# Three more waiting turns, and sample columns written by another engine, in a hybrid decoder step on one Trainium2 core

## The chip, the cores and the metric

The kernel runs on one core of a Trainium2 chip. A core has a matrix engine (TensorE, PE in the profile), a vector engine (VectorE, DVE), a scalar engine (ScalarE, ACT), a general engine (GpSimd, POOL), a queue engine that mostly issues transfers (SyncE, SP), and DMA engines that move data between the device memory and the on-chip buffers. The metric is the device time of one execution in microseconds; lower is better.

## What is computed

One inference step of one decoder layer, for 256 prompt tokens of a new sequence and 32 sample tokens (8 sequences of 4 tokens) with cached state. The two are held side by side as 288 columns.

```python
h = rms_norm(x, norm_mix_pre)
p_rwkv, lru_x, lru_g, q, k, v = split(h @ w_in)          # 2048 -> 5888 columns
y_a = rwkv7_mix(p_rwkv, ...)      # 8 heads of 64, matrix state per head
y_b = rglru_mix(lru_x, lru_g, ...)  # gated linear recurrence, width 512
y_c = attend(q, k, v)             # 8 heads of 128, three dilated windows; the sample tokens
                                  # also read a cache of 2048 keys and values per sequence
x = x + rms_norm(concat(y_a, y_b, y_c) @ w_out, norm_mix_post)
f = square(relu(rms_norm(x, norm_ffn_pre) @ ffn_w1)) @ ffn_w2
x = x + rms_norm(f, norm_ffn_post)
```

Also returned are the new states, and the keys and values of the new tokens.

## The kernel before

**The weight stream.** All weights pass once, as 382 chunks of 512 KB: 94 of `w_in`, 32 of `w_out`, 256 of the two feed-forward matrices. For a chunk, SP issues a load into one of RW = 4 buffers `w32` (L383); ACT rounds it into one of RH = 3 slots of `ring_h` (L393); DVE subtracts to get the rest in `ring_l` (L394, called the split here); PE runs 24 products of 128x288 (L429, L430, L431 in turn). SP, ACT and DVE run ahead of PE by at most these buffers: a split for chunk n waits until chunk n - 3 is used.

**The side work.** All else of the mixing stage (RWKV, recurrence, attention) is written as Python generators. `pump` advances each of them once per chunk, after 6 of 8 steps of its products; a `yield` waits for the next turn, and its value is a cost that counts towards a budget. So a number of `yield`s is a distance in chunks between what stands before and behind it. Behind this the Tile scheduler places each instruction in the one fixed order of its engine. Each engine then runs its own list in order, and an instruction that waits holds all behind it.

**The work around the change.**
- `gen_inv(hf)` inverts small triangular blocks, for two halves of the RWKV heads. DVE does 15 steps (L855, L857), copies (L860), and SP takes the result through device memory: two stores (L863), and eight loads with 64-byte runs into `TQ` (L868). `gen_mats` waits for `R["TQ"]` to be set and multiplies by it (L897).
- `evac_qkv` takes a finished head of q, k or v from the accumulator: DVE scales all 288 columns into a tile (L1314), then GpSimd copies the 32 sample columns of it into a collecting tile `qs`, `ks` or `vs` (L1315). `evac_lru` has GpSimd fill the leading columns of the convolution input (L1179, L1180).
- `gen_sample_scores` multiplies the sample queries by the cached keys: 32 loads `in_kc` of 896 KB by GpSimd (L1376), two at a time to products (L1408). Each load is tied behind `S["mark"]`, the latest copy into a collecting tile, in the order only. Two stream buffers in `arm` hold the keys.
- `gen_sample_soft(g)` scales the sample probabilities (DVE, L1437) and transposes them on PE (L1445). `gen_sample_pv` multiplies by the cached values: 32 loads `in_vc` (L1472) to products (L1494), 56 for a pair of loads. `more_streams` adds two more buffers from the arena (called `ar` and `arx` in the profile) as soon as there is room.
- `gen_prompt_attn` does the prompt's scores (L1561, L1562), softmax (L1565 to L1579) and transposes (L1585).

Of the kernel before, what the change touches and what calls it, by code (L numbers as in the profile page):

```python
# [12 lines left out]
ALU = mybir.AluOpType  # L13
# [298 lines left out]
def build(tc, A, O):  # L312
    nc = tc.nc
    sy, dv, ac, po, pe = nc.sync, nc.vector, nc.scalar, nc.gpsimd, nc.tensor
    with ExitStack() as ctx:
# [10 lines left out]
        rs_in = cp.tile([128, NT], F32, name="rs_in")  # L326
# [16 lines left out]
        def pvc(name, i=0, n=1):  # L343
            o, _ = PV[name]
            return pv[:, o + i:o + i + n]
# [89 lines left out]
        def must(*dims, **kw):  # L435
            n = 0
            while True:
                t = arena.get(*dims, **kw)
                if t is not None:
                    return t  # L440
                n += 1
                if n > 50:
                    raise RuntimeError("arena full")
                pump(100)
# [139 lines left out]
        S = {}  # L584
# [6 lines left out]
        def aw(*dims, **kw):  # L591
            while True:
                t = arena.get(*dims, **kw)
                if t is not None:
                    return t
                yield 0

        def bk(n=1):
            while len(banks.b) < n:
                yield 0  # L600
            return [banks.get() for _ in range(n)]
# [230 lines left out]
        def gen_inv(hf):  # L832
            R = RS[hf]
            while "MA1" not in R:
                yield 0
            dm = dp.tile([128, 512], F32, name=f"dm{hf}")
            do = dp.tile([8, 16, 256], F32, name=f"do{hf}")
            TQ = yield from aw(16, 64, top=True)
            po.memset(TQ, 0.0)
            W = yield from aw(4, 16, 16, top=True)  # L840
            Dm, Ti, Qi, tmp = (W[0:64, i] for i in range(4))
            for j in range(2):
                sy.dma_start(out=dm[:, 256 * j:256 * j + 256].rearrange("p (h t) -> p h t", h=4), in_=R["MA%d" % j][:, :, 0])
            po.memset(Ti, 0.0)
            d = Ti[:, 0, 0:1]
            po.memset(bass.AP(tensor=d.tensor, offset=d.offset, ap=[list(d.ap[0]), [17, 16]]), 1.0)
            d = dm[0:1, 0:1]
            for cb_ in range(8):
                sy.dma_start(out=Dm[8 * cb_:8 * cb_ + 8],
                             in_=bass.AP(tensor=d.tensor, offset=d.offset + 16 * 512 * cb_ + 16 * (cb_ % 4),  # L850
                                         ap=[[64, 8], [512, 16], [1, 16]]))
            yield 0
            for t in range(1, 16):
                v = tmp.rearrange("p a b -> p (a b)")[:, 0:t * t].rearrange("p (c s) -> p c s", c=t)
                dv.tensor_tensor(out=v, in0=Dm[:, 0:t, t].unsqueeze(1).to_broadcast([64, t, t]),  # L855
                                 in1=Ti[:, 0:t, 0:t].rearrange("p s c -> p c s"), op=ALU.mult)
                dv.tensor_reduce(out=Ti[:, t, 0:t], in_=v, axis=mybir.AxisListType.X, op=ALU.add)  # L857
                if t % 5 == 0:
                    yield 0
            dv.tensor_copy(out=Qi, in_=Ti.rearrange("p t s -> p s t"))  # L860
            for i, src in enumerate((Ti, Qi)):
                d = do[0:1, 0:1, 0:1]
                sy.dma_start(out=bass.AP(tensor=d.tensor, offset=d.offset + 8 * 256 * i, ap=[[16 * 256, 8], [256, 8], [1, 256]]),  # L863
                             in_=src.rearrange("p a b -> p (a b)"))
            for cb_ in range(8):
                c, b4 = cb_ // 4, cb_ % 4
                d = do[cb_:cb_ + 1, 0:1, 0:1]
                sy.dma_start(out=TQ[16 * cb_:16 * cb_ + 16, :, 16 * b4:16 * b4 + 16],  # L868
                             in_=bass.AP(tensor=d.tensor, offset=d.offset, ap=[[16, 16], [256, 16], [1, 16]]))
            arena.put(W)  # L870
            R["TQ"] = TQ
            yield 0

        def gen_mats(hf, j):
            R = RS[hf]
# [300 lines left out]
        def evac_lru(i, ps):  # L1176
            if i < 4:
                t = must(XW)
                po.memset(t[:, 0:3], 0.0)  # L1179
                po.tensor_copy(out=t[:, 259:283], in_=pvc("conv", 24 * i, 24))  # L1180
                dv.tensor_tensor(out=t[:, 3:259], in0=ps[:, 0:256], in1=rs_in[:, 0:256], op=ALU.mult)
                dv.tensor_tensor(out=t[:, 283:315], in0=ps[:, 256:288], in1=rs_in[:, 256:288], op=ALU.mult)
                sy.dma_start(out=O["o_conv_p"][:, i], in_=t[:, 256:259])
                sy.dma_start(out=O["o_conv_s"][:, i], in_=t[:, 291:315])
                xbt[i] = t
            else:
                t = must(NT)
                dv.tensor_tensor(out=t, in0=ps, in1=rs_in, op=ALU.mult)
                gbt[i - 4] = t
# [120 lines left out]
        def evac_qkv(which, i, ps):  # L1310
            if i == 0:
                S[which + "s"] = must(8, NS)
            t = must(NT)
            dv.tensor_tensor(out=t, in0=ps, in1=rs_in, op=ALU.mult)  # L1314
            S["mark"] = po.tensor_copy(out=S[which + "s"][:, i], in_=t[:, 256:288])  # L1315
            QKV[which, i] = t
            if which == "v":
                S["late"] = True
            S[which + "n"] = i + 1
            if which != "q":  # L1320
                sy.dma_start(out=O["o_" + which][:, i], in_=t)
# [108 lines left out]
        def gen_sample_soft(g):  # L1430
            SS = S["SS"]
            st_ = yield from aw(4)
            dv.tensor_reduce(out=st_[:, 0:1], in_=SS[:, g], axis=mybir.AxisListType.X, op=ALU.max)
            dv.tensor_scalar(out=st_[:, 0:1], in0=st_[:, 0:1], scalar1=-1.0, scalar2=None, op0=ALU.mult)
            ac.activation(out=SS[:, g], in_=SS[:, g], func=AF.Exp, bias=st_[:, 0:1], accum_out=st_[:, 1:2])
            dv.reciprocal(out=st_[:, 2:3], in_=st_[:, 1:2])
            dv.tensor_scalar(out=SS[:, g], in0=SS[:, g], scalar1=st_[:, 2:3], scalar2=None, op0=ALU.mult)  # L1437
            PT = yield from aw(8, 128)
            yield 0
            for half in range(2):  # L1440
                b, = yield from bk(1)
                for q in range(4):
                    kt = 4 * half + q
                    n = 128 if kt < 7 else 32
                    pe.transpose(b[0:n, 128 * q:128 * q + 128], SS[:, g, 128 * kt:128 * kt + n], ident)  # L1445
                if half == 0:
                    ac.activation(out=PT[:, 0:4], in_=b.rearrange("p (a b) -> p a b", a=4), func=AF.Copy)
                else:
                    ac.activation(out=PT[:, 4:7], in_=b[:, 0:384].rearrange("p (a b) -> p a b", a=3), func=AF.Copy)
                    ac.activation(out=PT[0:32, 7], in_=b[0:32, 384:512], func=AF.Copy)  # L1450
                banks.put(b)
                yield 0.5
            arena.put(st_)
            S["PT%d" % g] = PT

        def gen_sample_pv():
# [18 lines left out]
            for g in range(2):  # L1475
                while "PT%d" % g not in S:
                    yield 0
# [57 lines left out]
        def gen_prompt_attn():  # L1535
# [14 lines left out]
            for h0 in range(0, 8, 2):  # L1550
# [28 lines left out]
                    dv.tensor_scalar(out=PF[:, e, sl], in0=P[:, e, sl, ::-1], scalar1=s_[:, 8 + i:9 + i], scalar2=None, op0=ALU.mult)  # L1579
                yield 1.4  # L1580
                PT = yield from aw(2, 3, 128)
                bs = yield from bk(2)
                for e in range(2):
                    for i in range(3):
# [41 lines left out]
        for hf in range(2):  # L1626
            gens += [gen_rwkv(hf), gen_form(hf), gen_inv(hf), gen_mats(hf, 0), gen_mats(hf, 1), gen_chain(hf), gen_gn(hf)]
        gens += [gen_lru()]

        def evac_in(s, ps):  # L1630
            i = ORDER[s]
            if i < 14:
                evac_rwkv(i, ps)
            elif i < 22:
                evac_lru(i - 14, ps)
            else:
                w, h = "qkv"[(i - 22) // 8], (i - 22) % 8
                if "att" not in S:
                    S["att"] = True
                    gens.extend([gen_sample_scores(), gen_sample_pv(), gen_prompt_attn(), gen_prompt_pv()])  # L1640
                evac_qkv(w, h, ps)
# [92 lines left out]
        ps = psm.tile([128, NT], F32, name="mm", tag="mm")  # L1734
# [84 lines left out]
        ps = psm.tile([128, NT], F32, name="mm", tag="mm")  # L1819
# [3 lines left out]
        ps = psm.tile([128, NT], F32, name="mm", tag="mm")  # L1823
# [26 lines left out]
```

## Time and profile before

| | |
|---|---|
| median of 3 runs | 1458.4 us (1455.09, 1458.4, 1458.5) |
| profiled execution | 1457.43 us, of which 1455.4 us span and 2.0 us outside it |
| mean granted TensorE clock | 0.985 |
| busy share of the span | PE 97%, DVE 57%, ACT 41%, POOL 5% |
| mixing stage with side work | chunks 0 to 123, to about 610 us |
| products of a chunk on PE | 24, 0.133 us apart, so 3.2 us |
| cached key load, cached value load | 7.3 us and 7.3 to 8.9 us from issue to landing (medians) |

Read it so: PE is busy nearly all the time, with one dense stream of products, so a microsecond is gained or lost only where PE stands still, or runs at a lower granted clock. The feed-forward part after 620 us is dense and is not touched by the change.

### The profile page before, as it was taken

To read this page: it belongs to the slowest core of one execution; us is meant where nothing else is said; L and a number is where in the kernel's file an instruction comes from. 1 tells how busy PE (TensorE), PEld (TensorE's weight loads), DVE (VectorE), ACT (ScalarE), POOL (GpSimd) and SP (SyncE) were. 2 spreads that over 40 slices of the span, in tenths; PEclk is the share of its full clock that TensorE was granted. 3 is DMA by queue.
4 is the path that set the end of the run, shared out by engine and by line. 5 is a ranking of instruction groups with operands and counts; after the bars stand their busy time and mean duration, and the time that the engine had idled before them with its cause. 6 is when DMAs were issued, how large, how long until landed. Compare 5 with 4: busy or idle time off the path is not lost.

```text
span 1455.4 us, 28004 instructions
## 1 busy us (share of the span) xinstructions
PE 1415.3 (97%) x11730; PEld 1342.6 (92%) x11730; DVE 834.7 (57%) x1399; ACT 595.9 (41%) x866; POOL 67.5 (5%) x159
## 2 busy tenths in 40 slices
PE   8998999899999999999999999999999999999995
PEld 8898877787788999999999999999999999999995
DVE  7795486734586756695533355544455444454555
ACT  7432422333244533664443444433344333444442
POOL 1101011111111100000000000000000000000000
PEclk9999999899999999999999999999999999999998
DMA  8546366667778974434454444444445444454442
GB/s 294 185 152 196 124 235 224 225 244 258 269 263 332 321 281 163 158 125 166 159 170 164 166 168 161 171 162 169 164 162 171 161 171 163 165 169 161 171 161 80
DMA packets 86046, 276.62 MB, mean 190 GB/s; under 512 B 22384, under 2 KB 26016, under 8 KB 83872
## 3 DMA queue, kind: packets, MB, share of 16 engines
q1 hardware_dynamic: 75136, 212.23, 42.7%
q0 software_dynamic: 9920, 60.83, 11.3%
q8 instruction: 92, 1.51, 0.4%
q10 hardware_dynamic: 864, 1.77, 0.4%
q14 instruction: 34, 0.28, 0.1%
HBM read 267.97 MB, written 6.84 MB: 189 GB/s over the span
## 4 chain that ended last, share of the span: by engine, by line
PE 70%; issue 2%; DVE 2%; DMA 2%; ACT 1%; POOL 0%; DVEq 0%; POOLq 0%
PE mm L429 22%; PE mm L431 22%; PE mm L430 22%; DMA arm<-in_vc 1%; PE bt L1494 1%; DMA arm<-in_kc 1%; PE bt L1408 0%; DVE arm L1827 0%; DVE arx L1828 0%; PE bt L425 0%; DVE ring_l L394 0%; ACT ring_h L393 0%; DMA w<-in_w_out 0%; PE bt L1612 0%; ACT L1277 0%
## 5 line engine op out<-in xcount | busy, mean ns | idle before, releaser
L394 DVE TENSOR_TENSOR ring_l<-w,ring_h 128x1024 fp32r<-128x1024 f32 (+1 forms) x382 | 465.0, 1218 | 389.7 <-ACT ring_h L393 388.9
L393 ACT ACTIVATE ring_h<-w 128x1024 fp32r<-128x1024 f32 (+1 forms) x382 | 402.9, 1055 | 593.0 <-PE mm L430 523.7
L429 PE MATMUL mm<-hh,ring_h 128*128 128x288 f32 x1984 | 598.7, 302 | 4.8 <-ACT ring_h L393 3.0
L431 PE MATMUL mm<-hh,ring_l 128*128 128x288 f32 x1984 | 592.1, 299 | 0.8 <-DVE ring_l L394 0.8
L430 PE MATMUL mm<-hl,ring_h 128*128 128x288 f32 x1984 | 592.3, 299 | 0.2 <-DVE hl L548 0.2
L429 PEld LDWEIGHTS mm<-hh,ring_h 128*128 128x128 f32 x1984 | 373.7, 188 | 15.9 <-issue 7.1
L431 PEld LDWEIGHTS mm<-hh,ring_l 128*128 128x128 f32 x1984 | 374.8, 189 | 9.7 <-issue 5.5
L430 PEld LDWEIGHTS mm<-hl,ring_h 128*128 128x128 f32 x1984 | 374.4, 189 | 8.7 <-issue 5.8
L430 PE MATMUL mm<-fl,ring_h 128*128 128x288 f32 x1024 | 302.1, 295 | 0.0
L431 PE MATMUL mm<-fh,ring_l 128*128 128x288 f32 x1024 | 301.9, 295 | 0.0
L429 PE MATMUL mm<-fh,ring_h 128*128 128x288 f32 x1024 | 300.3, 293 | 0.0
L429 PEld LDWEIGHTS mm<-fh,ring_h 128*128 128x128 f32 x1024 | 192.5, 188 | 0.0
L430 PEld LDWEIGHTS mm<-fl,ring_h 128*128 128x128 f32 x1024 | 192.5, 188 | 0.0
L431 PEld LDWEIGHTS mm<-fh,ring_l 128*128 128x128 f32 x1024 | 192.4, 188 | 0.0
L1795 ACT ACTIVATE fh<-ft 128x288 fp32r<-128x288 f32 x64 | 28.3, 444 | 78.9 <-DVE ft L1794 78.9
L1803 DVE TENSOR_TENSOR arm<-mm,arm 128x288 f32<-128x288 f32 x48 | 22.0, 458 | 51.2 <-PE mm L431 51.2
L1796 DVE TENSOR_TENSOR fl<-ft,fh 128x288 fp32r<-128x288 f32 x64 | 29.2, 458 | 29.1 <-ACT fh L1795 29.1
L1408 PE MATMUL bt<-arm,ar 128*32 128x448 f32 x256 | 28.0, 546 | 2.6 <-DMA arm<-in_kc 2.3
L1794 DVE SCALAR_TENSOR_TENSOR ft<-mm,rt 128x288 f32<-128x288 f32 x63 | 28.3, 450 | 0.0
L1793 ACT ACTIVATE rt<-mm 128x288 f32<-128x288 f32 x63 | 24.9, 395 | 0.4 <-PE mm L431 0.4
L1702 DVE TENSOR_TENSOR ar<-mm,ar 128x288 f32<-128x288 f32 x32 | 14.5, 454 | 11.5 <-PE mm L431 11.5
L1376 POOL DMA_DIRECT2D arm<-in_kc x32 | 17.0, 531 | 70.2 <-PE bt L1408 61.4
(376 smaller groups left out, 906.9 us busy)
## 6 DMA issues: line engine op xcount, KB each, us to landing
w<-in_w SPq DMA_DIRECT2D x256, 512.0 KB
w<-in_w_in SPq DMA_DIRECT2D x91, 512.0 KB
arm<-in_kc POOLq DMA_DIRECT2D x32, 896.0 KB, 7.3
w<-in_w_out SPq DMA_DIRECT2D x32, 512.0 KB
arm<-in_vc POOLq DMA_DIRECT2D x8, 1024.0 KB, 7.4
ar<-in_vc POOLq DMA_DIRECT2D x8, 1024.0 KB, 7.3
arm<-in_vc POOLq DMA_DIRECT2D x9, 768.0 KB, 8.8
arx<-in_vc POOLq DMA_DIRECT2D x7, 768.0 KB, 8.9
```

Of the source, the lines that this page charges most:

```text
L393: ac.activation(out=h[:, lo:hi], in_=t[:, lo:hi], func=AF.Copy)
L394: dv.tensor_tensor(out=l[:, lo:hi], in0=t[:, lo:hi], in1=h[:, lo:hi].bitcast(F32), op=ALU.subtract)
L429: pe.matmul(out=ps, lhsT=h, rhs=xh, start=start, stop=False)
L430: pe.matmul(out=ps, lhsT=h, rhs=xl, start=False, stop=False)
L431: pe.matmul(out=ps, lhsT=l, rhs=xh, start=False, stop=stop)
L1376: after(po.dma_start(out=t, in_=A["kc"][seq[i]]), S["mark"])
L1408: pe.matmul(out=bh[32 * h:32 * h + 32, 0:448], lhsT=qz[:, h, b], rhs=t[:, h], start=(b == 0), stop=(b == NB - 1))
L1793: ac.activation(out=r, in_=ps, func=AF.Relu)
L1794: dv.scalar_tensor_tensor(out=f, in0=ps, scalar=0.0, in1=r, op0=ALU.max, op1=ALU.mult)
L1795: ac.activation(out=fh[:, m], in_=f, func=AF.Copy)
L1796: dv.tensor_tensor(out=fl[:, m], in0=f, in1=fh[:, m].bitcast(F32), op=ALU.subtract)
L1803: dv.tensor_tensor(out=facc[:, m], in0=ps, in1=facc[:, m], op=ALU.add)
```

## The change

It does five things. The numbers of waiting turns: in `gen_inv`, three turns pass between the issue of the loads of `TQ` and the setting of `R["TQ"]`, where before it was set at once; in `gen_sample_soft`, two turns rather than one between the scaling and the transposes; in `gen_prompt_attn`, one turn more between the scalings and the transposes. The engines: the leading columns of `evac_lru` are written by DVE; and the sample columns in `evac_qkv` are a second product by DVE straight from the accumulator, no longer a copy by GpSimd of the scaled tile, so that `S["mark"]` is now a DVE instruction.

```diff
@@ gen_inv @@
             arena.put(W)
+            for _ in range(3):
+                yield 0
             R["TQ"] = TQ
-            yield 0
@@ evac_lru @@
                 t = must(XW)
-                po.memset(t[:, 0:3], 0.0)
-                po.tensor_copy(out=t[:, 259:283], in_=pvc("conv", 24 * i, 24))
+                dv.memset(t[:, 0:3], 0.0)
+                dv.tensor_copy(out=t[:, 259:283], in_=pvc("conv", 24 * i, 24))
@@ evac_qkv @@
             dv.tensor_tensor(out=t, in0=ps, in1=rs_in, op=ALU.mult)
-            S["mark"] = po.tensor_copy(out=S[which + "s"][:, i], in_=t[:, 256:288])
+            S["mark"] = dv.tensor_tensor(out=S[which + "s"][:, i], in0=ps[:, 256:288], in1=rs_in[:, 256:288], op=ALU.mult)
@@ gen_sample_soft @@
             PT = yield from aw(8, 128)
-            yield 0
+            for _ in range(2):
+                yield 0
@@ gen_prompt_attn @@
                 PT = yield from aw(2, 3, 128)
+                yield 0
                 bs = yield from bk(2)
```

What this does to the order of the engines is shown at three places. Line numbers of the changed kernel are higher by 1 behind L868, by 2 behind L1437 and by 3 behind L1581. A place on PE is given as the number of chunks whose products stand before it: 58.00 is behind 58 times 24 of them.

**The first key loads on GpSimd.** `ar_88` and `arx` are tiles of the arena; L1392 spreads the sample queries. Before:

```order
L1315 COPY arx<-arx 128x32
L1392 COPY ar_88<-arx 128x8x4
L1315 COPY arx<-arx 128x32
L1376 DMA arm<-in_kc 128x1792 x2
L1392 COPY ar_88<-arx 128x8x4
```

After the change, in the same place:

```order
L615 COPY ar_88<-pv 128x8
L1393 COPY ar_88<-arx 128x8x4
L1377 DMA arm<-in_kc 128x1792 x2
L1393 COPY ar_88<-arx 128x8x4 x3
L1377 DMA arm<-in_kc 128x1792 x8
```

The first two loads stood behind two copies L1315 and now stand behind the first L1393 alone; eight more follow without a copy between them. On PE the first key products move from 40.33 to 38.54, the second pair from 42.83 to 39.58. The first products with `TQ` (L897, now L898) stay at 34.75.

**PE at chunk 58.** Before, one run of side products with no weight product between them:

```order
L431 MATMUL mm<-hh,ring_l 128x288
L1445 MATMUL bt<-ca,arx 128x128 x4
L897 MATMUL bt<-ar_88 64x64 x16
L1561 MATMUL bt<-ar_88,arx 128x128
L1562 MATMUL bt<-ar_88,arx 128x256
L1561 MATMUL bt<-arx 128x128
L1562 MATMUL bt<-arx 128x256
L429 MATMUL mm<-hh,ring_h 128x288
```

After the change, what stands at 57.83:

```order
L431 MATMUL mm<-hh,ring_l 128x288
L1409 MATMUL bt<-arm,ar_88 32x448 x4
L898 MATMUL bt<-ar_88 64x64 x8
L429 MATMUL mm<-hh,ring_h 128x288
L430 MATMUL mm<-hl,ring_h 128x288
L431 MATMUL mm<-hh,ring_l 128x288
L429 MATMUL mm<-hh,ring_h 128x288
L430 MATMUL mm<-hl,ring_h 128x288
L898 MATMUL bt<-ar_88 64x64 x8
```

The transposes L1447 now come at 55.54 and 55.79, the prompt's transposes at 56.54 and 56.75, the prompt's scores L1563 from 58.25 on; key products now stand at 57.21 and 57.83, and a pair of value products at 56.21.

On DVE, the part just ahead of this place. Before, between two splits (L394, of the chunks 53 and 54):

```order
L394 TENSOR_TENSOR ring_l<-w_2345,ring_h 128x1024
L1138 SCALAR_TENSOR_TENSOR ar_88<-bt,ar_88 128x288 x2
L1149 RECIPROCAL ar_88<-ar_88 128x288 x2
L1120 TENSOR_TENSOR ar_88<-bt,ar_88 128x512
L1150 TENSOR_TENSOR ar_88<-ar_88 128x576
L1122 TENSOR_TENSOR ar_88<-ar_88 128x512
L1153 TENSOR_SCALAR ar_88<-ar_88,pv 128x288 x2
L1114 TENSOR_TENSOR ar_88<-ar_88,ca 128x512
L1155 TENSOR_TENSOR ar_88<-ar_88 128x576
L778 TENSOR_TENSOR ar_88<-bt,ar_88 128x288
L855 TENSOR_TENSOR ar_88<-ar_88 64x1
L394 TENSOR_TENSOR ring_l<-w_2397,ring_h 128x1024
```

After the change, the start of a run of 42 instructions without a split, behind which the next split stands:

```order
L394 TENSOR_TENSOR ring_l<-w_2306,ring_h 128x1024
L1150 RECIPROCAL ar_88<-ar_88 128x288
L855 TENSOR_TENSOR ar_88<-ar_88 64x1
L1121 TENSOR_TENSOR ar_88<-bt,ar_88 128x512
L857 TENSOR_REDUCE ar_88<-ar_88 64x1
L1150 RECIPROCAL ar_88<-ar_88 128x288
L855 TENSOR_TENSOR ar_88<-ar_88 64x4
L1123 TENSOR_TENSOR ar_88<-ar_88 128x512
L857 TENSOR_REDUCE ar_88<-ar_88 64x2
L1151 TENSOR_TENSOR ar_88<-ar_88 128x576
```

The inverse's steps now lie among the reciprocals and scalings, and ten of its fifteen pairs stand in this run; before, one.

**The value loads on GpSimd.** Before, where the third and fourth buffer come in (`ar_88`, `arx`; a buffer of `arm` is one of the first two):

```order
L1472 DMA ar_88<-in_vc 128x2048
L1376 DMA arm<-in_kc 128x1792 x2
L1179 MEMSET arx 128x3
L1472 DMA arm<-in_vc 128x1536
L1472 DMA arm<-in_vc 128x2048
L1179 MEMSET arx 128x3
L1180 COPY arx<-pv 128x24
L1472 DMA arx<-in_vc 128x1536
```

After the change:

```order
L1474 DMA arm<-in_vc 128x2048
L1474 DMA arm<-in_vc 128x1536
L1474 DMA ar_88<-in_vc 128x2048
L1474 DMA arm<-in_vc 128x2048
L1474 DMA arm<-in_vc 128x1536 x2
L1474 DMA arm<-in_vc 128x2048
L1474 DMA ar_88<-in_vc 128x1536
```

All ten value loads ahead of these rows' third go to `arm`; the third buffer is first taken by the row with `ar_88`. Before, the pairs of value products stood at 59.00, 74.88, 78.21, 79.83, 80.46, 80.71, 81.75 and then every two chunks; now at 56.21, 73.88, 75.33, 78.58, 81.12, 82.50 (its second part at 82.88), 83.08 (second part 83.17), 84.75 and then every two chunks.

## Rows read from the trace of the kernel before

**Rows 1.** The page: busy time by engine; a group of instructions by line.

```profile
PE 1415.3 (97%) x11730; PEld 1342.6 (92%) x11730; DVE 834.7 (57%) x1399; ACT 595.9 (41%) x866; POOL 67.5 (5%) x159
...
L394 DVE TENSOR_TENSOR ring_l<-w,ring_h 128x1024 fp32r<-128x1024 f32 (+1 forms) x382 | 465.0, 1218 | 389.7 <-ACT ring_h L393 388.9
```

**Rows 2.** Waits of PE: in total us, times, longest us.

```profile
PE bt L897 <- DMA ar<-do: 4.3, 1, 4.3
PE bt L1494 <- DMA ar<-in_vc: 3.1, 1, 3.1
PE mm L429 <- ACT ring_h L393: 3.0, 3, 1.6
...
PE bt L1494 <- DMA arm<-in_vc: 1.1, 1, 1.1
```

**Rows 3.** Windows: length; PE, PEld, DVE, ACT, POOL busy; clock, DMA share, GB/s.

```profile
0.00:10.00 10.00, 6.07 (x31) 5.32 (x32) 3.24 (x6) 5.14 (x9) 2.81 (x20) 1.00 0.80 262
...
130.00:140.00 10.00, 5.68 (x42) 5.36 (x41) 2.91 (x3) 1.51 (x2) 1.09 (x4) 0.90 0.84 255
140.00:150.00 10.00, 10.00 (x75) 8.99 (x76) 4.25 (x7) 3.27 (x3) 1.30 (x2) 0.76 0.43 156
280.00:290.00 10.00, 6.39 (x45) 4.71 (x46) 5.11 (x12) 1.59 (x3) 0.21 (x1) 0.57 0.46 162
290.00:300.00 10.00, 9.95 (x141) 9.03 (x141) 4.35 (x13) 4.12 (x13) 1.29 (x3) 0.92 0.31 105
430.00:440.00 10.00, 6.71 (x109) 5.48 (x107) 7.15 (x11) 2.82 (x5) 1.08 (x3) 0.92 0.90 346
440.00:450.00 10.00, 9.07 (x114) 8.23 (x115) 5.47 (x19) 5.33 (x7) 2.45 (x6) 0.74 0.98 381
```

**Rows 4.** Timeline of PE at 139 us: start, length, idle before it.

```profile
139.41 0.44 PE L897 MATMUL bt<-ar 64*64 64x64 f32 x2 [4.32 <-DMA ar<-do]
```

**Rows 5.** Timeline of POOL, 120 to 130 us.

```profile
121.26 1.48 POOL L1392 COPY ar<-arx 128x32 f32<-128x32 f32 x1
128.22 1.15 POOL L1315 COPY arx<-arx 128x32 f32<-128x32 f32 x1 [5.48 <-DVE arx L1314]
129.31 1.06 POOL L1376 DMA_DIRECT2D arm<-in_kc  x2
```

**Rows 6.** Timeline of SP's queue, 126 to 142 us.

```profile
131.11 4.89 SPq L868 DMA_DIRECT2D ar<-do  x8
```

**Rows 7.** DMA queues, 134 to 136 us: packets, MB, share (q0 GpSimd's, q1 SP's).

```profile
q0 software_dynamic: 132, 0.83, 99.9%
q1 hardware_dynamic: 56, 0.01, 2.4%
```

**Rows 8.** The same, 277 to 280 us, while the other half's TQ is loaded.

```profile
q1 hardware_dynamic: 1592, 0.10, 34.5%
```

**Rows 9.** Timeline of PE at chunk 58, 281 to 290 us.

```profile
281.04 0.88 PE L1445 MATMUL bt<-ca,arx 128*128 128x128 f32 x4 [1.98 <-DVE arx L1437]
282.67 1.29 PE L897 MATMUL bt<-ar 64*64 64x64 f32 x16 [0.75 <-ACT ar L1447]
284.54 1.12 PE L897 MATMUL bt<-ar 64*64 64x64 f32 x16 [0.59 <-DVE ar L898]
286.19 0.80 PE L1561 MATMUL bt<-ar,arx 128*128 128x128 f32 x2 [0.53 <-DVE ar L898]
...
288.56 0.79 PE L1561 MATMUL bt<-arx 128*128 128x128 f32 x2 [0.71 <-DVE ar L1565]
```

**Rows 10.** Timeline of PE, a pair of value products, 427 to 430 us.

```profile
427.43 1.08 PE L1494 MATMUL bt<-ar 128*32 128x128 f32 x32
```

**Rows 11.** Timeline of POOL: the first load that refills this pair's buffers.

```profile
428.84 0.53 POOL L1472 DMA_DIRECT2D ar<-in_vc  x1 [7.88 <-PE bt L1494]
```

**Rows 12.** The line L1472, all of its 32 loads, issue to landing.

```profile
DMA to landing us min/median/max: 4.8/8.0/11.4
```

**Rows 13.** The window with the work around chunk 58.

```profile
250.00:300.00 50.00, 45.12 (x390) 37.85 (x392) 34.70 (x90) 16.69 (x35) 6.59 (x16) 0.90 0.59 203
```

## The prediction

> **What bounds the kernel now.** The page first: PE is busy 97% of the span, no other engine comes near it [rows 1]. So the question is where PE stood still and where its clock was lower. The waits of PE give the first [rows 2]: one of 4.3 us for `TQ`, 3.1 and 1.1 us for cached values; the 3.0 us for `ring_h` lie at the start, which the change doesn't touch. [...]
>
> *Stall A, TQ.* 4.32 us idle up to 139.41 [rows 4]; of the 6.8 us at half speed, 0.6 + 4.8 = 5.4 lie behind it, and half of that is lost: 2.7. Together 7.0 us.
>
> *Stall B, chunk 58.* Side products with no weight product between them, each waiting for the one before through DVE or ACT: 1.98 + 0.75 + 0.59 + 0.53 + 0.71 = 4.6 us idle [rows 9]. Of the 10.2 us at half speed some 2.6 are those idle gaps, 7.6 are work, which costs 3.8. Together 8.4 us.
>
> *Stall C, values.* 3.1 + 1.1 us idle [rows 2]; 5.7 of the 6.8 us at half speed are work, 2.8 lost. Together 7.0 us.
>
> That is 22.4 us, and no more than this can come from these places.
>
> **Stall A.** Why was TQ late? SP issued its eight loads from 131.11 for 4.89 us [rows 6], yet the product ran at 139.41. Two key loads of 0.9 MB had been issued at 129.31 [rows 5]. From 134 to 136 us GpSimd's queue had 99.9% of the DMA engines and SP's moved 56 packets [rows 7]; at the other half's TQ, with no key load about, it moved 1592 packets in 3 us [rows 8], 531 per us. Eight loads are 8 x 256 = 2048 runs of 64 bytes, 3.9 us at that rate. The change takes the key loads away from there: they had waited for the copy L1315 of 128.22, which had waited 5.48 us for DVE [rows 5], and now stand behind the first L1393. As L1392 that ended at 122.74; so they issue some 6.5 us earlier and are through (landing 8 us for the like [rows 12], so 131) when TQ's loads begin. With 3.9 us and 1 to 2 us to issue and land, TQ is there at 136 to 137, and the first L898 stays where it was on PE. I take 137: idle 1.9 rather than 4.3. The two turns added to `gen_inv` do nothing at this place.
>
> Does the clock fall after 1.9 us? It fell after 1.98 at chunk 58, where 0.75 and more idle followed [rows 9]; it didn't after the 1.6 us for `ring_h` at the start [rows 2, 3]. Here dense work follows; I take that it stays. Then A costs 1.9: **-5.1 us**. If it falls, -2.4.
>
> [...]
>
> **Key products.** They now stand at 38.54 and 39.58: 1.04 chunks, 3.3 us, and the first pair's own products and others apart, about 7.5 us by the PE order. With two buffers a load issues when its buffer's products are done, 1.4 and 2 us after a pair begins (so 427.43 to 428.84 for values [rows 10, 11]), and lands 4.8 to 11.4 us later, 8.0 in the median [rows 12]. The second pair is late by 0 to 2 us: **+0.7**.
>
> **Chunk 58.** The pile is spread: 8.4 us gone. In its place DVE gets a run of 42 instructions without a split. By the mean of DVE here, 34.70 us for 90 instructions [rows 13], it is 16.2 us, and the split behind it 1.2 [rows 1]. PE has three chunks in the ring (9.6 us), and some 4 us of other products stand between; the split comes 17.4 - 13.8 = 3.6 us late. It is 0 if the ring is full and short steps overlap, 6.7 if one chunk of the ring is missing when the run starts. With a fall of the clock like A's (2.4) that is 6. A pair of key loads stands behind the value products of 56.21 and is late by 0 to 4, I take 1.7. So 7.7 for 8.4: **-0.7**, from -7 to +5.
>
> **Values.** The third buffer now comes late, and three pairs stand close: from the one at 81.12 to 82.50 are 1.38 chunks, 4.4 us, and its own 56 products, 1.8 by 1.08 for 32 [rows 10]: 6.2 us; its first refill needs 1.4 + 5.9 = 7.3 (between the 4.8 and 8.0 of [rows 12]): 1.1 late. The second needs about 10 and its products stand 9.4 behind: 0.6. The fourth load of the group follows into the first's buffer and stands only 0.7 chunks behind: 2.8. That is 4.5, and some 2 for a fall of the clock: 6.5 for 7.0, **-0.5**, from -5 to +12.
>
> **What costs nothing.** 24 instructions of 32 columns and eight small ones are new on DVE, at 0.2 us or so some 6 us over 400; DVE is idle 31% of the time even around chunk 58 [rows 13], and the ring's three chunks cover it. Without that cover it is part of the run above. GpSimd loses the copies; it is busy 5% [rows 1]. The weight products are the same.
>
> **The sum**, on the profiled execution's 1457.4 (1.0 below the median of the runs): 1457.4 - 5.1 + 0.7 - 0.7 - 0.5 = 1451.8, so 1452.
>
> **The rivals.**
> 1. *The clock falls at A all the same*, since 1.9 us is between the wait that kept it and the one that didn't, or the two stores L863 ahead of the loads of `TQ` now meet the key loads and land later. 1457.4 - 2.4 + 0.7 - 0.7 - 0.5 = 1454.5. Chance 0.20.
> 2. *The key loads were not what held TQ*: its 64-byte packets are slow to start whatever else runs. A stays at 7.0: 1456.9. For it: the change leaves the first L898 and SP's loads where they were. Against it: [rows 7, 8]. Chance 0.10. [...]
> 3. *DVE's run isn't late*, because its short steps fill one another's gaps: then chunk 58 costs the 1.7 of the key loads alone, 6.0 less: 1445.8. For it: 34.70 busy of 50 there [rows 13]. Chance 0.20.
> 4. *The two-buffer refills fall behind.* If landings around chunk 82 are near the 11.4 of [rows 12] rather than 6 to 8, the three waits are 3.2, 1.5 and 6.5 us, and each brings a fall of the clock like C's (2.4 to 2.8): 19 us for 7.0. 1457.4 - 5.1 + 0.7 - 0.7 + 12 = 1464.3, slower. It decides from 17 us on; the stretch has DMA at 0.90 to 0.98 already [rows 3]. Chance 0.20.
>
> **How the numbers follow.** The forecast has 0.30, the rivals 0.70. What a measurement of this kernel can tell from no change is about 0.3%, 4.4 us: 1454.0 to 1462.8 about the median. The forecast is 2 us beyond this, so a sixth of it goes to no change, with rivals 1 and 2 (0.30 less some of the first that falls under 1454): faster 0.46, same 0.33, slower 0.21. The range 1444 to 1464 reaches from rival 3 to rival 4, and leaves out what lies beyond both, and a gain at all three stalls (1436).
>
> **What would show it.** Right: GpSimd's first key loads at 122 to 124 us; PE's wait for `TQ` under 2 us with the clock at 1.00 from 130 to 150; no waits for L1437 and L1565; a wait for `ring_l` or `ring_h` of some us near chunk 54, 262 to 275 us; waits for `in_vc` near chunk 82 to 83. Wrong: a `TQ` wait of 4 us with the key loads gone from 131 to 136 (rival 2); no ring wait (rival 3); `in_vc` waits over 10 us in sum (rival 4); a wait at a place that has none now.

## The result, and the profile after

The changed kernel takes 1447.0 us (median of 4 runs, 1445.7 to 1448.6) against 1458.45; the ratio is 0.9926, with a 95% interval of 0.9907 to 0.9945. So it is faster by 0.55 to 0.93%. The forecast was 1452; the way and the range were right, the gain of 11 us was larger than the 6 forecast. The profiled execution took 1447.71 us, with a span of 1445.6, that is 9.8 under the one of before.

The waits of PE first (total us, times, longest us), then the windows that answer to [rows 3] (length; PE, PEld, DVE, ACT, POOL busy; clock, DMA share, GB/s):

```profile
PE bt L1496 <- DMA arm<-in_vc: 3.5, 1, 3.5
PE mm L429 <- ACT ring_h L393: 2.8, 3, 1.7
PE mm L429 <- ACT hh L547: 1.8, 1, 1.8
PE bt L1409 <- DMA arm<-in_kc: 1.7, 1, 1.7
PE bt L898 <- DMA ar<-do: 1.5, 1, 1.5
...
PE bt L1496 <- DMA ar<-in_vc: 1.1, 1, 1.1
PE bt L1421 <- DVE ar L1316: 1.0, 1, 1.0
```

```profile
130.00:140.00 10.00, 8.52 (x65) 8.25 (x63) 3.98 (x5) 2.76 (x3) 0.25 (x1) 1.00 0.63 189
140.00:150.00 10.00, 10.00 (x137) 8.53 (x136) 4.17 (x9) 5.06 (x8) 0.25 (x1) 1.00 0.43 160
...
250.00:260.00 10.00, 8.40 (x55) 7.34 (x54) 9.51 (x34) 5.30 (x12) 0.00 (x0) 0.90 0.18 53
260.00:270.00 10.00, 9.62 (x59) 7.65 (x57) 8.66 (x23) 4.38 (x8) 2.33 (x4) 0.93 0.43 139
...
430.00:440.00 10.00, 6.57 (x74) 5.42 (x75) 4.26 (x11) 3.62 (x5) 1.00 (x2) 0.66 0.81 312
```

Read against [rows 2, 3]: the wait for `TQ` is 1.5 us, not 4.3, and the clock stays at 1.00 from 130 to 150. No wait for the sample scaling (L1437, now L1438) is left in the list, and of those for L1565 (now L1567) only 0.2 us at another place: the pile at chunk 58 stands no more. The wait for cached values is still there, 3.5 and 1.1 us, with the clock at 0.66 behind it.

The place of `TQ`, in the timelines of GpSimd, SP's queue and PE, and then in the queue table for 134 to 136 us, to be set against [rows 4 to 7]:

```profile
122.95 1.06 POOL L1377 DMA_DIRECT2D arm<-in_kc  x2
...
133.32 3.77 SPq L868 DMA_DIRECT2D ar<-do  x8
...
136.75 0.30 PE L898 MATMUL bt<-ar 64*64 64x64 f32 x2 [1.48 <-DMA ar<-do]
```

```profile
q1 hardware_dynamic: 1026, 0.07, 34.4%
```

The two key loads go out at 122.95, 6.4 us earlier. SP's loads begin 2.2 us later than before. The stores ahead of them (L863) now share the DMA engines with the key loads, which have 78.4% of them from 127 to 131 us; in the run below that moves only the key loads back, SP's loads begin at 131.00 again. Yet from 134 to 136 SP moves 1026 packets where it had moved 56, and PE goes on at 136.75, not at 139.41. PE begins chunk 36 at 142.67 us; before, at 147.70.

Chunks 54 to 58, in the timeline of PE (what each waited for):

```profile
256.50 0.25 PE L1421 MATMUL bt<-ar,arx 128*32 128x32 f32 x2 [0.97 <-DVE ar L1316]
257.63 0.40 PE L431 MATMUL mm<-hh,ring_l 128*128 128x288 f32 x1 [0.42 <-DVE ring_l L394]
270.26 0.40 PE L429 MATMUL mm<-hh,ring_h 128*128 128x288 f32 x1 [0.64 <-ACT ring_h L393]
270.97 0.40 PE L431 MATMUL mm<-hh,ring_l 128*128 128x288 f32 x1 [0.18 <-DVE ring_l L394]
279.00 0.96 PE L1409 MATMUL bt<-arm,ar 128*32 128x448 f32 x8 [1.73 <-DMA arm<-in_kc]
```

The long run of DVE is late, as forecast, but by little: 0.97 us at a product (L1421) that needs one of the new sample columns (L1316), a place that had no wait, and 0.42 at the ring, at 257.63 rather than between 262 and 275. The 0.64 and 0.18 us at 270 have another cause: there ACT's L393 stands behind ACT's copies of the transposes (L1449 to L1452, from 266.96 to 269.00) and begins at 269.15. The pair of key loads behind the value products of 56.21 is late by 1.73.

### The profile page after: what moved, and what is told of

Same layout as the page of the kernel before. It is cut to its first block, busy times and chain, and to the rows that moved or that the text cites. A ratio compares the mean times of both kernels' runs of the same rounds, so it can differ in the third digit from the quotient of the medians.

```text
span 1445.6 us, 27979 instructions
## 1 busy us (share of the span) xinstructions
PE 1412.0 (98%) x11730; PEld 1340.2 (93%) x11730; DVE 836.5 (58%) x1431; ACT 600.2 (42%) x870; POOL 63.3 (4%) x127
## 3 DMA queue, kind: packets, MB, share of 16 engines
q8 instruction: 92, 1.51, 0.4%
## 4 chain that ended last, share of the span: by engine, by line
PE 82%; issue 7%; DMA 6%; DVE 4%; POOL 1%; ACT 0%; SPq 0%; POOLq 0%; DVEq 0%; ACTq 0%
PE mm L429 25%; PE mm L431 25%; PE mm L430 25%; DMA arm<-in_vc 2%; DMA arm<-in_kc 2%; PE bt L1409 1%; DVE ring_l L394 1%; PE bt L1496 1%; DMA ar<-in_vc 1%; DMA w<-in_w_in 0%; DVE arm L1830 0%; DMA do<-ar 0%; DVE arx L1831 0%; DVE hl L548 0%; PE bt L898 0%
## 5 line engine op out<-in xcount | busy, mean ns | idle before, releaser
L394 DVE TENSOR_TENSOR ring_l<-w,ring_h 128x1024 fp32r<-128x1024 f32 (+1 forms) x382 | 464.9, 1218 | 385.2 <-ACT ring_h L393 382.7
L393 ACT ACTIVATE ring_h<-w 128x1024 fp32r<-128x1024 f32 (+1 forms) x382 | 402.6, 1055 | 587.2 <-PE mm L430 538.9
L1496 PE MATMUL bt<-arm,ar 128*32 128x128 f32 x648 | 22.6, 287 | 3.5 <-DMA arm<-in_vc 3.5
L1496 PEld LDWEIGHTS bt<-arm,ar 128*32 128x32 f32 x648 | 17.8, 114 | 6.6 <-DVE ar L1290 3.7
```

The costliest lines, as they stand in the source:

```text
L393: ac.activation(out=h[:, lo:hi], in_=t[:, lo:hi], func=AF.Copy)
L394: dv.tensor_tensor(out=l[:, lo:hi], in0=t[:, lo:hi], in1=h[:, lo:hi].bitcast(F32), op=ALU.subtract)
L1496: pe.matmul(out=bb[32 * h:32 * h + 32, 0:128], lhsT=PT[:, kt, 32 * h:32 * h + 32], rhs=t[:, q, h], start=(kt == 0), stop=(kt == 6))
```

## The experiments

A number behind each run says by how much PE began chunk 36 (behind `TQ`) and chunk 104 (behind all of the side work that moves) earlier or later than in the kernel before, taken from the profiled executions of both. For the changed kernel they are -5.0 and -9.8 us. Where PE's order is the same, waits can be compared one by one; where it isn't, only chunk 104 and the medians. A fall of the clock is given as time at half speed: one minus the granted clock of a window, times its 10 us, times two. That the clock goes to half is read from the window of 280 to 290 us in the next run, which lies wholly in a fall and shows 0.50. (Chunks are counted on PE. There are 380 of them, 92 of `w_in`; the 382 of L394 in [rows 1] come from two chunks that are split in halves.)

**Only the engines.** The edits of `evac_lru` and `evac_qkv` (only the second is shown), with the turns of before.

```diff
-            S["mark"] = po.tensor_copy(out=S[which + "s"][:, i], in_=t[:, 256:288])
+            S["mark"] = dv.tensor_tensor(out=S[which + "s"][:, i], in0=ps[:, 256:288], in1=rs_in[:, 256:288], op=ALU.mult)
```

> Of the change only the engines: sample columns of q, k, v and the convolution's leading columns by DVE, with the turns of before. PE's order keeps TQ's first products at 34.75 and the pile at 58.00. Theory (the key loads held TQ, and it is the move off GpSimd that takes them away; the turns only spread chunk 58): TQ's wait 1 to 2 us with the clock at 1.00 from 130 to 150, the pile at 58 still some 8 us, about 5 us under the kernel before: 1451 to 1455. Rival (the turns do all of it): as before, 1456 to 1460.

1448.5 us, ratio 0.9934 (0.9918 to 0.995); chunk 36 -5.1, chunk 104 -9.1. Better than the theory said: nearly the whole gain is here. `TQ` waits 1.5 us. The pile at 58 is as before and a little longer (four more transposes in it), here in the timeline of PE, and in the windows:

```profile
274.62 0.66 PE L1445 MATMUL bt<-ca,arx 128*128 128x128 f32 x4 [1.93 <-DVE arx L1437]
...
277.91 1.12 PE L897 MATMUL bt<-ar 64*64 64x64 f32 x16 [0.59 <-DVE ar L898]
...
284.28 1.12 PE L1445 MATMUL bt<-ca,arx 128*128 128x128 f32 x4 [0.72 <-DVE ar L1565]
```

```profile
270.00:280.00 10.00, 6.16 (x59) 5.27 (x58) 5.95 (x11) 3.01 (x5) 0.00 (x0) 0.82 0.61 166
280.00:290.00 10.00, 8.57 (x38) 6.78 (x41) 4.60 (x18) 2.39 (x10) 0.00 (x0) 0.50 0.04 15
```

But no wait for cached values or keys is left in the run: the same edits moved the value pairs in PE's order to 73.79, 77.12, 77.46, 78.29, 79.75 and 81.75, and stall C is gone. The theory had not priced that. The run is 1.5 us behind the changed kernel, and their intervals overlap: what the turns add to the engines can't be told from nothing.

**Only the turns.** The three edits in `gen_inv`, `gen_sample_soft` and `gen_prompt_attn`.

```diff
+            for _ in range(3):
+                yield 0
             R["TQ"] = TQ
-            yield 0
...
-            yield 0
+            for _ in range(2):
+                yield 0
...
                 PT = yield from aw(2, 3, 128)
+                yield 0
```

> Of the change only the three numbers of turns; GpSimd copies as before. PE's order is that of the changed kernel, GpSimd's begins as before, with the first key loads behind the second sample copy. Theory: TQ's wait stays at 4 us and more with the fall of the clock, the pile at 58 is gone, about 5 us under the kernel before: 1451 to 1455. Rival (the turns do all): 1445 to 1449.

1455.25 us, ratio 0.9981 (0.997 to 0.9992); chunk 36 -0.6, chunk 104 -0.3. The half on `TQ` came out as the theory said (4.5 us of wait, and a fall of the clock). The pile is gone and has brought next to nothing, because other groups wait in its place, and the clock falls for 3.4, 3.4 and 6.8 us between 252 and 294:

```profile
PE bt L898 <- DMA ar<-do: 4.5, 1, 4.5
...
PE bt L1409 <- DMA arm<-in_kc: 2.8, 1, 2.8
PE bt L1496 <- DMA arm<-in_vc: 2.5, 1, 2.5
PE bt L777 <- DVE ar L857: 2.4, 1, 2.4
...
PE mm L431 <- DVE ring_l L394: 1.4, 2, 1.2
```

**Without the inverse's turns.** The changed kernel with `R["TQ"]` set at once and one turn behind it.

```diff
-            for _ in range(3):
-                yield 0
             R["TQ"] = TQ
+            yield 0
```

> The changed kernel with the setting of TQ as before (at once, and one turn behind it). TQ's first products stay at 34.75; a pile of side products stands again, at 60.00. Theory: the gain at TQ stays, the pile costs again some 8 us with a fall of the clock: 1451 to 1456. Rival (the two softmax turns spread the pile, the inverse's add nothing): 1445 to 1449.

1466.5 us, ratio 1.0067 (1.0046 to 1.0088), slower than the kernel before; chunk 36 -5.8, chunk 104 +8.4. Both missed. `TQ` keeps its gain, and a pile stands at 60.00 that is far larger than the one of 58: transposes of prompt and sample, value products, three groups with `TQ`, scores and key products, a dozen groups, each waiting 0.5 to 0.8 us for the one before. Two of them from the timeline, and the windows, where the clock falls for (0.37 + 0.33 + 0.49) x 20 = 24 us:

```profile
289.33 0.49 PE L910 MATMUL bt<-ar 64*64 64x64 f32 x4 [0.80 <-ACT ar L915]
292.11 3.21 PE L1495 MATMUL bt<-arm,ar 128*32 128x128 f32 x56 [0.75 <-ACT ar L915]
```

```profile
280.00:290.00 10.00, 6.02 (x58) 4.49 (x60) 1.89 (x3) 3.18 (x8) 0.00 (x0) 0.63 0.24 87
290.00:300.00 10.00, 7.12 (x137) 5.86 (x135) 1.20 (x3) 1.05 (x3) 1.07 (x2) 0.67 0.40 136
300.00:310.00 10.00, 7.92 (x54) 3.83 (x52) 3.88 (x16) 2.25 (x9) 0.88 (x2) 0.51 0.25 76
```

Behind the pile PE waits 3.0 us for DVE at 368.18 and 4.2 at 443.62, each with a fall of the clock; the loss is not the pile's alone. In this order, then, the turns of the two softmaxes need those of the inverse: without them they send more work to one place.

**Key loads late.** One number in `gen_sample_scores` of the changed kernel; PE's order is the same.

```diff
-                    if S.get("qn", 0) >= 2:
+                    if S.get("qn", 0) >= 3:
                         pre(LAG)
```

> The changed kernel with one thing altered: the first two key loads may be issued from the third head of q on, not from the second (the 2 in the condition ahead of pre(LAG) is a 3). PE's order is unchanged; on GpSimd the two loads move behind the second L1393, which waits for DVE until about 128. Theory (contention with TQ's small packets): TQ lands 2 to 4 us later, PE waits 4 us with the clock falling: 5 us over the changed kernel, 1450 to 1454. Rival (it was GpSimd's copies or DVE's work that delayed TQ, not the transfer): as the changed kernel, 1445 to 1449.

1451.7 us, ratio 0.9955 (0.9942 to 0.9967); chunk 36 +1.2, so 6.2 us later than in the changed kernel, of which 2.8 are made up by chunk 104: its clock doesn't fall behind its waits at 263 and 438. The sample columns are still DVE's and GpSimd has no copies; only the two loads stand later, and stall A is back:

```profile
129.55 1.06 POOL L1377 DMA_DIRECT2D arm<-in_kc  x2
...
131.00 5.32 SPq L868 DMA_DIRECT2D ar<-do  x8
...
140.27 0.44 PE L898 MATMUL bt<-ar 64*64 64x64 f32 x2 [4.89 <-DMA ar<-do]
```

```profile
q1 hardware_dynamic: 50, 0.04, 5.9%
```

The last row is from the queue table for 134 to 136 us. The theory holds: with the copies gone from GpSimd and DVE's work unchanged, the place of the transfer alone decides.

**Without the prompt's turn.**

```diff
                 PT = yield from aw(2, 3, 128)
-                yield 0
                 bs = yield from bk(2)
```

> The changed kernel without the extra turn in the prompt's attention. PE's order keeps the spread at chunk 58 (no pile), and the value pairs stand at 73.79, 75.17, 77.42, 80.00, 80.75, 82.75 and then every two chunks, so only one pair follows another within a chunk. Theory (what is left of the changed kernel's stalls is the crowd of value pairs at 81.12 to 83.17, and a turn more or less only moves the crowd): the wait for cached values falls from 4.6 us with its fall of the clock to 1 to 3 us, 1440 to 1446. Rival (the prompt's turn is what took the scaling's wait from PE): a wait for L1579's scalings of 1 us or more at each of the four transposes, 1449 to 1454.

1445.5 us, ratio 0.9919 (0.9904 to 0.9933); chunk 104 -12.3. As the theory said: one wait for cached values of 1.7 us and no fall of the clock there; no wait for the scalings. A new wait stands elsewhere, 1.8 us for DVE's L857 ahead of L777, with the clock at 0.95 and 0.88 behind it. It looks like stall A over again at a second place. Ahead of it SP loads the inverse's input with 64-byte runs (L849), and DVE's L855 reads what it loads. The timelines of SP's queue, GpSimd and DVE in this run; the transfer that the last row names is not the one that L855 reads:

```profile
237.51 3.03 SPq L849 DMA_DIRECT2D ar<-dm  x8
238.98 0.53 POOL L1474 DMA_DIRECT2D arm<-in_vc  x1 [9.01 <-PE bt L1409]
246.85 0.15 DVE L855 TENSOR_TENSOR ar<-ar 64x1 f32<-64x1 f32 x1 [2.37 <-DMA o_k<-ar]
```

The same in the changed kernel, where L855 doesn't wait:

```profile
236.09 2.86 SPq L849 DMA_DIRECT2D ar<-dm  x8
239.12 0.53 POOL L1474 DMA_DIRECT2D arm<-in_vc  x1 [9.54 <-PE bt L1409]
```

The large load goes out 1.5 us into SP's 3.0 us in the one, 0.2 us behind them in the other. In all four runs with a wait at L777, of 1.8 to 2.4 us (this one, only the turns, one turn placed ahead, and no prompt turn with one pair spread), a large load was issued during SP's loads or up to 1.1 us ahead of them, and DVE waited 2.4 to 2.9 us. In the changed kernel and the five runs with its order up to this place it came 0.1 to 0.4 us behind them, and nothing waited; in the other three kernels the two meet as well, but DVE asks for the result later. No run moves this load alone, so that it is the cause here is argued from these cases and not shown. The prompt's turn buys nothing.

**Without the sample softmax's turn.**

```diff
             PT = yield from aw(8, 128)
-            for _ in range(2):
-                yield 0
+            yield 0
```

> The changed kernel without the extra turn in the sample softmax. In PE's order the transposes stand at 55.50 and 57.04, the second half's products with TQ from 58.12, no pile at 58; the value pairs stand at 57.38, 60.17, 76.79, 77.58, 80.12, 81.08, 81.83, 83.75. Theory (no turn by itself buys anything; what counts is whether PE's order has a pile or a crowd): within 5 us of the changed kernel, 1443 to 1452, its waits for cached values at 77 to 82. Rival (the softmax's turn removes the wait for L1437): a wait of PE for the scaling of 1 us or more at 55.50, 1450 to 1455.

1455.9 us, ratio 0.9985 (0.9971 to 0.9999); chunk 36 -5.1, chunk 104 -3.1. Outside what either expected: there is no wait for L1437, but the order has put the second half's `TQ` products and two groups of key products where their loads aren't there yet, each with a fall of the clock of 3.4 us (timeline of PE):

```profile
283.41 0.67 PE L898 MATMUL bt<-ar 64*64 64x64 f32 x14 [2.80 <-DMA ar<-do]
300.38 1.20 PE L1409 MATMUL bt<-arm,ar 128*32 128x448 f32 x8 [2.84 <-DMA arm<-in_kc]
313.12 0.96 PE L1409 MATMUL bt<-arm,ar 128*32 128x448 f32 x8 [1.74 <-DMA arm<-in_kc]
```

**Value pairs spread.** The changed kernel, with one line of `gen_sample_pv` altered.

```diff
-                    for _ in range(2):
+                    for _ in range(3 if g == 0 and b in (4, 5) else 2):
                         yield from take()
                         pre(i + 2 + LAG)
```

> The changed kernel with one thing altered: the fifth and sixth value pair take three chunks of credit rather than two. PE's order up to 82.50 is unchanged; the pair of 82.50 stands at 82.75 and 82.88, the next at 84.75 rather than 83.08, and each later pair two chunks later. Theory (the stall is the crowd of pairs on two buffers, and the load that is late is the first of the pair of 82.50): the wait for that first load falls from 3.5 to 2 to 3 us, the one of 1.1 at 83.17 goes, the clock falls less or not: 2 to 5 us under the changed kernel, 1442 to 1445. Rival (the loads are late because the DMA engines are full, whatever the order): the same 4 to 5 us of waits, 1446 to 1449.

1445.1 us, ratio 0.9919 (0.9902 to 0.9935); chunk 36 -3.7, chunk 104 -13.0. In between: the first wait of the crowd is hardly shorter, 3.3 us at 434.17 (the list of waits names DVE's L1290 for it), the second, of 1.1 in the changed kernel (at 449.67, in the pair of 84.75, not at 83.17 as expected), is 0.2, and the clock falls for 3.4 us rather than 6.8 (0.83 from 430 to 440). From chunk 36 on it gains 4.5 us on the changed kernel's profiled execution, of the 2 to 5 expected; but at `TQ` its clock fell (0.88 and 0.95), which the changed kernel's profiled execution was spared, and the medians differ by 1.9 with intervals that overlap.

**The convolution's columns on GpSimd again.**

```diff
-                dv.memset(t[:, 0:3], 0.0)
-                dv.tensor_copy(out=t[:, 259:283], in_=pvc("conv", 24 * i, 24))
+                po.memset(t[:, 0:3], 0.0)
+                po.tensor_copy(out=t[:, 259:283], in_=pvc("conv", 24 * i, 24))
```

> The changed kernel with the convolution's leading columns written by GpSimd again. PE's order is the same in all places named. Theory (this part of the change does nothing): 1446 to 1449. Rival (GpSimd's memset and copy between the value loads delay them): 1 to 3 us more wait for cached values, 1449 to 1452.

1445.3 us (1443.4 to 1449.7), ratio 0.9922 (0.99 to 0.9944). No difference from the changed kernel can be told, in four executions that lie up to 6 us apart: this part has no effect that these runs show.

**One turn, placed ahead.** The engines' run with the order of two lines changed.

```diff
             arena.put(W)
+            yield 0
             R["TQ"] = TQ
-            yield 0
```

> The run with only the engines changed, and in the inverse the one turn of before placed ahead of the setting of TQ rather than behind it. That alone takes the pile from 58 in PE's order: the transposes stand at 56.54 and 60.00, the second half's products with TQ from 57.83 to 59.00, the prompt's scores at 59.21 and 59.67; a smaller pile (scores, key products, a transform) stands at 62.00; value pairs at 78.62, 79.54, 79.75, 81.75. Theory (the pile at 58 is worth some 8 us, and the engines' run had nothing else left): 3 to 8 us under the engines' run, 1440 to 1445. Rival (each order finds its own place to wait, the sum of side work with waits stays): 1446 to 1451.

1451.6 us, ratio 0.9954 (0.9937 to 0.997); chunk 104 -7.6. The theory fell, the rival is nearer: the pile at 58 is gone and the time is some 3 us longer than with it, with intervals that overlap; the 3 to 8 us of gain are not there. PE waits 2.8 us ahead of a transpose (L1447), 1.8 ahead of L777, 1.5 ahead of L1002, and the clock falls at 287 for 3.4 us and at 330 to 350 (0.92 and 0.56), a place that had no stall of this size.

**No prompt turn, one pair spread.** The run without the prompt's turn, and the fifth pair with three chunks of credit (`3 if g == 0 and b == 4 else 2`).

> The changed kernel without the prompt's turn, and the fifth value pair of the first group taking three chunks of credit rather than two, so that the pairs stand at 80.00, 81.75, 83.75 and every two chunks: no pair follows another within a chunk and a half. PE's order before 80 is that without the prompt's turn. Theory (crowd of value pairs): its wait of 1.7 us for cached values at 80.75 goes, 1 to 3 us under the run without the prompt's turn: 1442 to 1445. Rival (DMA is full there, the wait only moves): 1445 to 1447.

1443.6 us (1438.2 to 1445.4), ratio 0.9897 (0.988 to 0.9914); the lowest here. No wait for cached values is left (the one at L777 is, 2.0 us), and the clock stays up through the crowd's place:

```profile
430.00:440.00 10.00, 10.00 (x120) 9.64 (x119) 9.36 (x36) 7.14 (x8) 1.05 (x2) 1.00 0.97 377
440.00:450.00 10.00, 10.00 (x122) 9.26 (x124) 9.86 (x24) 2.91 (x4) 1.06 (x2) 1.00 0.96 337
```

With DMA at 0.97 and 0.96 and no wait, full DMA engines alone didn't make the stall here.

**The changed kernel again,** beside the last two.

> The changed kernel unaltered, beside the two others on the same chip: 1445 to 1449.

1447.2 us (1442.9 to 1450.0), ratio 0.9925 (0.991 to 0.9941). The run before it is 3.6 us under this one, on the same chip; their intervals against the kernel before overlap only from 0.991 to 0.9914.

The profiled execution of this run has PE's order and much the same waits as the first one of the changed kernel: 1.90 us for `TQ`, 0.97 and 0.42 at 258 and 259, 1.9 for keys, 3.2, 0.8 and 0.7 for values. But its clock falls at other places: for 3.4 us behind `TQ`, and not at 258 nor behind the 3.2 us, where the first execution had 3.4 and 6.8 us at half speed:

```profile
430.00:440.00 10.00, 5.96 (x114) 4.66 (x116) 6.18 (x19) 4.64 (x5) 1.52 (x3) 1.00 0.96 350
```

So in these runs a fall of the clock is not a fixed price of a place in the order; it came and went between two executions of one kernel.

## Why the prediction was right, point by point

**The price of a stall.** The 7.0, 8.4 and 7.0 us that the terms set out from are the idle time and half of the work's time at half speed (6.8, 10.2 and 6.8 us in the windows of [rows 3], with the gaps in them taken off). The half is an estimate that no run shows: the weight products behind the wait for `TQ`, in the kernel before, start 0.24 us apart at a clock of 0.50 (141.39, 141.63), against 0.133, so 1.8 times.

**Stall A: right in place, mechanism and size.** Forecast 1.9 us of wait with the clock kept, measured 1.48 with the clock kept; -5.1 forecast, -5.0 at chunk 36. The key loads went out at 122.95 (forecast 122.7). That the loads of `TQ` would stay where they were was wrong: they began 2.2 us later behind the stores, and made it up, PE needing only the first of them (136.75, while their issue runs to 137.09). The run with late key loads shows the cause: 50 packets in 2 us and 4.89 us of wait, with all else kept. Rival 2 is out; of rival 1 the later landing behind the stores came true, and cost nothing.

**Clock at A: right in the profiled execution, and by luck.** The same kernel run again had 1.90 us of wait, as much as forecast, and the clock fell there (0.90 and 0.93). That was rival 1's first half.

**Key products: +0.7 forecast, no wait at 39.58.** The term was mis-sized to the small side of its range. Unseen was that the key waits of before, 2.3 us in three places, went with the new order:

```profile
PE bt L1408 <- DMA arm<-in_kc: 2.3, 3, 1.1
```

The prediction has no term for this row. It is a cost of PE's order as the others are.

**Chunk 58: -0.7 forecast.** The replacing waits were forecast as 6 us at DVE's run and 1.7 at the keys. Measured: 0.97 + 0.20 at L1421, 1.24 at the ring, 1.73 at the keys, 4.1 us idle; the clock's 0.90 and 0.93 from 250 to 270 are 3.4 us at half speed, half of it lost. That is 5.8 for 8.4, -2.6. DVE's run was late, as the step said, but PE waited 0.97 + 0.42 = 1.4 us for it rather than 3.6: the 42 instructions took 13.6 us (242.76 to 256.38) and not 16.2, since the mean of the stretch is too high for them. Rival 3, that the run isn't late, was partly right.

**Values: -0.5 forecast.** Measured 3.54 + 1.10 idle and 6.8 us at half speed, 5.6 of it work: 7.4 for 7.0. The wait stands where it was put, at the pair of 82.50; but it is one long wait of 3.5 for the first refill and not three at this pair and the next (the 1.10 stands in the pair of 84.75). Its load went out at 424.98 and PE began at 433.43, 8.4 us, where 5.9 had been taken between the shortest and the median landing.

The terms measure -5.0 - 2.3 - 2.6 + 0.4 = -9.5; the span fell by 9.8. Against the forecast's -5.6 it is 3.0 more at the keys (a loss of 0.7 forecast, a gain of 2.3 measured), 1.9 more at chunk 58, and 0.9 less at the values. The keys are the step that failed most. That the number 1452 came within 5 us of the result owes something to luck: of its four terms only A's was right in size. The terms themselves are those of one execution: in the second one the clock gave back 1.7 us at 258 and 2.8 at the values, and took 1.7 at `TQ`.

**What no term held.** The runs with one part alone say more than the sum does. The engines' edits by themselves gave 9.8 us of median, the turns by themselves 3.0, both 11.4 (10.5 when measured again). The prediction read each part as the owner of one stall: the engines of A, the turns of the pile. In the runs, each part also changes PE's order behind it (the engines alone from 44.58 on), and whether three value pairs stand close, or a pile stands at 58 or 60, follows from all of them together. The engines alone lose stall A and stall C and lengthen B; adding the turns takes B down and brings C back. So 5 us of the gain have a cause that a run of its own shows, the place of the key loads; the rest is the balance of these waits, read from the traces and not isolated. Each order tried has its own waits; why the scheduler sets a pair at 82.50 in one and at 81.75 in the other was not looked into and stays open.

## What to carry to other kernels

A small transfer that something waits for should not share its time with a large one of another queue: when the two key loads moved away by 6 us, the wait behind 64-byte runs went from 4.3 to 1.5 us, and it came back, with 4.9, when only these loads were moved back. Turns, lags and other distances that a scheduler turns into an order had no worth of their own here; they are to be judged by the order that comes out, by where side products stand in a row without filler, and where buffers are asked for again in less than a load's time, and each combination is to be timed. Two small changes of such an order, chosen by that reading, took a further 3.6 us.

## What the runs showed of the hardware

The granted clock fell behind waits of PE shorter than the stalls of before, and not behind each of them. At the one wait for `TQ`, in a dense stream on both sides, the clock stayed at 1.00 from 130 to 150 us with waits of 0.87, 1.28, 1.4, 1.48, 1.51, 1.52 and 1.63 us; it fell with 1.59, 1.72 and 1.90, for 3.4 us at half speed, and with 4.32, 4.52 and 4.89 us (the kernel before, only the turns, key loads late) for 6.8, 3.4 and 6.8. Two of these, first with value pairs spread, then with no prompt turn and one pair spread:

```profile
136.54 0.29 PE L898 MATMUL bt<-ar 64*64 64x64 f32 x2 [1.59 <-DMA ar<-do]
130.00:140.00 10.00, 8.41 (x56) 8.14 (x55) 4.18 (x5) 2.44 (x3) 0.25 (x1) 0.88 0.62 191
...
136.72 0.30 PE L898 MATMUL bt<-ar 64*64 64x64 f32 x2 [1.63 <-DMA ar<-do]
130.00:140.00 10.00, 8.37 (x64) 8.10 (x62) 4.00 (x5) 2.58 (x3) 0.25 (x1) 1.00 0.62 187
```

So a wait of some 1.6 to 1.9 us cost 1.3 to 1.9 us more in one execution than a like one in another (chunk 36 at 144.43 us in the second execution of the changed kernel, 142.67 in the first). At other places the length decides as little: the clock stayed at 1.00 from 430 to 450 us behind waits for cached values of 3.0 us (key loads late) and 3.2 us (the second execution), and fell behind 0.97 and 0.42 in one execution of the changed kernel and not in the other. At a clock of 0.50 the weight products started 0.24 us apart, against 0.133: 1.8 times and not twice, so that the halves lost that are taken above are a little too large.

While GpSimd's load held 99.9% of the DMA engines (the kernel before, 134 to 136 us) and 94.0% (key loads late, the same stretch), SP moved 28 and 25 packets per microsecond (56 and 50 in 2 us); without it, 513 (the changed kernel, the same stretch) and 531 [rows 8]. That second rate is about the pace of issue (2048 runs in 3.8 us) and not a limit of the engines: in the kernel before, from 136 to 138 us, with all eight loads issued and GpSimd's nearly through, SP moved 1021 per microsecond:

```profile
q1 hardware_dynamic: 2042, 0.12, 88.9%
```

In these tables a packet of SP's loads is one 64-byte run (the 2042 are 0.12 MB). The wait for `TQ` was 2.8 us longer with the key loads about (4.32) than without (1.48). By what rule the DMA engines divided their time between the two queues is not shown: no run here varies the size of the packets.
